# The first convolution block's projection, made in two halves among the last pair's attention

## The chip, the cores and the metric

The kernel runs on one core of a Trainium2 chip. The metric is the device time of one execution in microseconds (us). The core's engines are PE (TensorE, matrix products; PEld is its weight loading), DVE (VectorE), ACT (ScalarE), POOL (GpSimd) and SP, whose queue issues most of the transfers. Each works through its own list of instructions in order and waits for the others by semaphores. PE's products go to PSUM, eight banks of 128 x 512 floats; everything else lies in SBUF.

## What is computed

One layer of a streaming encoder on a sequence of 1024 tokens of width 1024, all in float32. Cut to what matters here:

```
h = rmsnorm(x) * (1 + scale_m(c)) + shift_m(c)
z, xbc, dt, q, k, v = split(h @ W_in)
xbc = silu(causal_dwconv(xbc, conv_w) + conv_b)      # 1024 channels, 4 taps
y_s = mamba2_ssd(xbc, dt) * silu(z), normed          # 8 heads x 64
y_a = chunked_attention(q, k, v, rel_bias)           # 8 heads x 64, own chunk and 8 before
x = x + gate_m(c) * (concat[y_s, y_a] @ W_out)
x = x + gate_f(c) * conv_ffn(rmsnorm(x) * (1 + scale_f(c)) + shift_f(c))
out = rmsnorm(x)
```

The change concerns the first 128 of the channels of xbc that the kernel treats first (block 4 of eight blocks): their projection `h @ W_in`, and the convolution behind it.

## The kernel before

**Precision.** Matrix products are made in three parts for float32 accuracy: each operand is split into a high part (a copy in a reduced format, on ACT) and a low part (the difference, on DVE or POOL). `mm3` (L83 to L86) issues high by high, high by low and low by high. `split` (L88 to L94) makes the parts. The normed input lies transposed in SBUF for the whole first phase as `hH` and `hL`, two halves of 512 tokens.

**Projection.** `gemm_ft` (L665) multiplies one block of 128 output channels with all tokens: for each half of the tokens, eight steps over the width, three matmuls of 512 columns each, so 24 matmuls a half and 48 a block. `wu_pair` (L156) loads a block's weights into one of two `raws` buffers, and splits them into `wh` (two buffers) and `wl` (one of two halves of one buffer, taken in turn).

**Attention.** `attention(p)` (L637) treats heads in four pairs. A pair has four steps u of two blocks of 128 queries. `attn_scores` (L567) makes the scores of both heads of one block in two PSUM tiles `s` (two buffers of two banks in all), adds the bias and takes the row maximum on DVE (L581), the exponential on ACT (L584), the reciprocal of the sum on DVE (L586) and the scaling on POOL (L587), into tiles `p` (eight buffers). `attn_pv` (L591) turns p on PE (L613, L616, into `tp`, two banks), splits it (ACT and DVE, L93, L94), and multiplies it with v into `pv` (one bank); L629 and L630 add its two parts into `ya`.

**The filler.** Between a step's scores and its pv part, `attention` calls the functions that the table `GP` (L34) lists for the pair and the step: projections of the q, k and v of the pairs to come, by `gemm_part` (L674). They accumulate in the tile `acc`, one bank (L686), and `evac_qkv` (L232) takes the result out: for v by a copy on ACT into a p tile (L259), for q and k by ACT and DVE (L243, L250, L253). `GPIN` ties some of these matmuls behind certain scores. In pair 3 the steps 0 and 1 have filler (the second token halves of k and v of pair 3 itself), and the steps 2 and 3 have none. In the steps 1 and 2 of pair 3 the weights of the convolution blocks 4 and 6 are loaded and split ahead of time into `early` (L660).

**Convolution stage.** After attention `conv_silu(ft)` (L694) treats the eight blocks in the order 4, 6, 5, 7, 0, 1, 2, 3. It takes an `s` tile (both halves of the tokens, L696), makes the projection (L697), starts the convolution with the last tap on ACT (L699), adds three taps on DVE, reading the projection in PSUM (L701), and applies silu on ACT (L705). After each block `conv_mods` (L749) makes up to four columns of modulation: a 512 KB weight load on SP (L144) into `xs` or `wos`, and a product with a row `rowa` that is summed on DVE (L146). The tiles of this stage lie in SBUF where attention's lay. Later come the z projection (L847, weights by `wz_weights`, L832), the SSD scan, the output projection and the feed-forward part.

**rowb.** `rowb` (L106) is a row buffer of 1024 floats a partition, beside `rowa` in one tile. Early on it holds a diagonal and then the first pair's bias, later (L769) a row of gates. Between pair 0 and L769 nothing uses it.

**Order.** The order of instructions on each engine is planned when the program is built: the framework lays the program out on a simulated timeline (L1807), taking what stands earlier in the program first among what is ready, unless `tc.issue_after` ties an instruction behind another. So a change in the program may alter the order elsewhere too. In the trace, parts of attention's pv work lie as late as 311 us, among the convolution's matmuls.

Of the kernel before, what the change touches and what calls it, by code (L numbers as in the profile page):

```python
# [10 lines left out]
F32 = mybir.dt.float32  # L11
F32R = mybir.dt.float32r
AF = mybir.ActivationFunctionType
# [3 lines left out]
P = 128  # L17
# [13 lines left out]
BOTH, H0, H1 = (0, 1), (0,), (1,)  # L31
# [1 line left out]
        (3, 2, H1): {0: (3, 0), 3: (3, 1), 6: (3, 2)}}  # L33
GP = {1: {0: ((2, 0, BOTH), (2, 1, BOTH)), 2: ((2, 2, BOTH),)},  # L34
      2: {0: ((3, 0, BOTH), (3, 1, H0)), 2: ((3, 2, H0),)},
      3: {0: ((3, 1, H1),), 1: ((3, 2, H1),)}}
XL = (3, 4, 7, 7)
XS = (4, 6, 7, 7)
XM = (6, 7, 7, 7)
# [33 lines left out]
def tile_block(ctx: ExitStack, tc: tile.TileContext, x, ccol, pk, w_ada, w_first, w_ft, w_z,  # L73
               w_out, w_up, w_down, bias, fnw, out, dbg=None):
    nc = tc.nc
    V, A, T = (InOrder(tc, e) for e in (nc.vector, nc.scalar, nc.tensor))
# [6 lines left out]
    def mm3(ps, lh, ll, rh, rl, start, stop, more=False):  # L83
        T.matmul(ps, lh, rh, start=start, stop=False, skip_group_check=more)  # L84
        T.matmul(ps, lh, rl, start=False, stop=False, skip_group_check=more)  # L85
        T.matmul(ps, ll, rh, start=False, stop=stop, skip_group_check=more)  # L86

    def split(hi, lo, src, ehi, elo, scale=None):  # L88
        if scale is not None:
            A.activation(hi, src, AF.Copy, scale=scale)  # L90
            V.scalar_tensor_tensor(lo, src, scale, f32(hi), op0=ALU.mult, op1=ALU.subtract)
            return
        i = A.activation(hi, src, AF.Copy) if ehi is A else ehi.tensor_copy(hi, src)  # L93
        return i, elo.tensor_tensor(lo, src, f32(hi), ALU.subtract)  # L94
# [11 lines left out]
    rowa, rowb = rows_[:, 0, :], rows_[:, 1, :]  # L106
# [32 lines left out]
    def raw_tile(n=1024):  # L139
        rawc[0] += 1  # L140
        return raws[:, rawc[0] % 2, 0:n]
# [14 lines left out]
    def wu_pair(src, hieng, loeng):  # L156
        t = raw_tile()
        nc.sync.dma_start(t, src)
        wh = wu.tile([P, 1024], F32R, tag="wh", name="wh")
        if not wls:  # L160
            wls.append(wu.tile([P, 2, 1024], F32R, tag="w2", bufs=1, name="wl"))
        wl = wls[0][:, rawc[0] % 2, :]
        split(wh, wl, t, hieng, loeng)
        return wh, wl
# [8 lines left out]
    def ht(hh, kt):  # L173
        return hth[hh][:, :, kt, :], htl[hh][:, :, kt, :]

    def c4(ap):
        return ap.rearrange("p (a b) -> p a b", a=4)
# [9 lines left out]
    psv = es_p1.enter_context(tc.tile_pool(name="psv", bufs=1, space=PSUM, reuse_waits="tile"))  # L187
# [35 lines left out]
    def new_pair(p):  # L223
        qk[p] = {n: [qk_tile(F32R) for _ in range(2)] for n in ("q", "kh", "kl")}
        qk[p]["v"] = vv[:, :, p % 2]
# [6 lines left out]
    def evac_qkv(p, which, hh, ps, tmp, tps):  # L232
        d = qk[p]
        c = slice(hh * 512, hh * 512 + 512)
        up, dn = slice(64, 128), slice(0, 64)

        def move(dst, o, src, r, sc):
            nc.sync.dma_start(f32(dst[o, c]), f32(src[r, sc]))

        if which == 0:  # L240
            q0, q1 = d["q"]
            lo = ev_tile()
            A.activation(q0[:, c], ps, AF.Copy, scale=0.125)  # L243
            V.scalar_tensor_tensor(lo, ps, 0.125, f32(q0[:, c]), op0=ALU.mult, op1=ALU.subtract)
            move(q1, up, q0, up, c)
            move(q1, dn, lo, up, slice(0, 512))
            move(q0, up, lo, dn, slice(0, 512))
        elif which == 1:
            (kh0, kh1), (kl0, kl1) = d["kh"], d["kl"]
            A.activation(kh0[:, c], ps, AF.Copy)  # L250
            for o in (up, dn):
                move(kh1, o, kh0, up, c)
            V.tensor_tensor(kl0[:, c], ps, f32(kh0[:, c]), ALU.subtract)  # L253
            for o in (up, dn):
                move(kl1, o, kl0, up, c)
            for t in (kh0, kl0):
                move(t, up, t, dn, c)
        else:
            A.activation(tmp, ps, AF.Copy)  # L259
            for j in range(4):  # L260
                T.transpose(tps[:, j * P:(j + 1) * P], tmp[:, j * P:(j + 1) * P], ident)
            b = slice(4 * hh, 4 * hh + 4)
            tv = tps.rearrange("p (a h b) -> p a h b", a=4, h=2)
            split(d["v"][:, b, :, 0, :], d["v"][:, b, :, 1, :], tv, A, V)

    def s_tile():
        return ps1.tile([P, 1024], F32, tag="s", bufs=2, name="s")
# [283 lines left out]
    def p_tile():  # L551
        return pp.tile([P, 640], F32, tag="p", name="p")

    def tp_tile():
        return pst.tile([P, 512], F32, tag="tp", bufs=2, name="tp")
# [78 lines left out]
    last_v, last_g, early = [], [], {}  # L634
# [30 lines left out]
    def gemm_ft(wh, wl, outs, pins={}, hhs=BOTH):  # L665
        for hh in hhs:
            for kt in range(KT):
                w = slice(kt * P, (kt + 1) * P)
                with tc.issue_after(slast[pins[kt]]) if hh == hhs[0] and kt in pins else ExitStack():
                    mm3(c4(outs[hh]), wh[:, w], wl[:, w], *ht(hh, kt), kt == 0, kt == KT - 1)  # L670

    held = {}

    def gemm_part(p, which, hhs):  # L674
        if which == 0:
            new_pair(p)
        if which == 2 and hhs == H1:
            wh, wl = held.pop(p)
        elif p == 2 and which < 2:
            with tc.issue_after(wpin[0].ins), tc.issue_after(wpin[1].ins):  # L680
                wh, wl = wu_pair(w_ft[8 + 3 * (p - 2) + which], A, V)
        else:
            wh, wl = wu_pair(w_ft[8 + 3 * (p - 2) + which], A, G)
        if which == 2 and hhs == H0:
            held[p] = wh, wl
        outs = {hh: psv.tile([P, 512], F32, tag="acc", bufs=1, name="acc") for hh in hhs}  # L686
        gemm_ft(wh, wl, outs, GPIN.get((p, which, hhs), {}), hhs)
        for hh in hhs:
            tmp = tps = None
            if which == 2:  # L690
                tmp, tps = p_tile()[:, 0:512], tp_tile()
            evac_qkv(p, which, hh, outs[hh], tmp, tps)

    def conv_silu(ft, dst):  # L694
        wh, wl = early.pop(ft) if ft in early else wu_pair(w_ft[ft], A, V)
        ps = s_tile()  # L696
        gemm_ft(wh, wl, [ps[:, 0:512], ps[:, 512:1024]])  # L697
        w = [pkt[:, SCW + 4 * ft + j:SCW + 4 * ft + j + 1] for j in range(4)]
        A.activation(dst, ps, AF.Identity, scale=w[3], bias=pkt[:, SCB + ft:SCB + ft + 1])  # L699
        for j in range(1, 4):  # L700
            last = V.scalar_tensor_tensor(dst[:, j:S], ps[:, 0:S - j], w[3 - j], dst[:, j:S],  # L701
                                          op0=ALU.mult, op1=ALU.add)
        for hh in range(2):
            c = slice(hh * 512, hh * 512 + 512)
            A.activation(dst[:, c], dst[:, c], AF.Silu)  # L705
        return last.ins

    part = lambda *a: (lambda: gemm_part(*a))
    bias_early()
    attention(0)  # L710
# [53 lines left out]
    for g in range(2):  # L764
        conv_mods(2 * g + 1, conv_silu(4 + g, bt_[g]))
        if g == 1:
            V.tensor_tensor(gcol[:, 0:8], modc[:, G_M:G_M + 8], gbias[0], ALU.add)
            cols_to_dram(gcol[:, 0:8], tp_tile()[0:8, 0:P], th512()[0:8, 0:P], gmd)
            for t, k in ((rowb[:, 0:512], 0), (gm1, 4)):  # L769
                nc.sync.dma_start(t.rearrange("p (a b) -> p a b", a=4), rows_from(gmd, k, 4))  # L770
        conv_mods(2 * g + 2, conv_silu(6 + g, ct_[g]))
# [5 lines left out]
    for ft in range(4):  # L777
        xt = bcp.tile([P, S], F32, tag="rm", bufs=2, name="xst")
        conv_mods(5 + ft, conv_silu(ft, xt))
        for hh in range(2):  # L780
            tps = tp_tile()
            for j in range(4):
                T.transpose(tps[:, j * P:(j + 1) * P], xt[:, (4 * hh + j) * P:(4 * hh + j + 1) * P],
                            ident)
            A.activation(xs[:, 4 * hh:4 * hh + 4, ft * P:(ft + 1) * P],
                         tps.rearrange("p (a b) -> p a b", a=4), AF.Copy)
# [698 lines left out]
    bufs = {}  # L1485
# [325 lines left out]
```

## Time and profile before

| | |
|---|---|
| median of 3 runs | 1171.44 us (1170.91 to 1171.88) |
| the profiled execution itself | 1171.69 us, span 1170.0 us |
| DVE, ACT, POOL busy | 78%, 50%, 13% of the span |
| chain that ended last, by engine | PE 86%, DVE 9%, ACT 3%, issue 2% |
| DMA packets | 64029, 169.15 MB, mean 145 GB/s |
| projection of block 4 on PE | from 248.07 to 262.25 us, in `s`, among pv work |
| its convolution on DVE | from 264.77 to 269.28 us |

The span runs from the first to the last instruction of the profiled execution. A line of the trace names start and duration in us, engine, line of the kernel, operation, and what is written from what. In a list of groups the number after "x" counts instructions, then come the busy time in us and the mean of one in ns, then the idle time of the engine just before them. In a list of waits, the engine and line that waited stand first, then the releaser, the time in all, how often, and the longest. A matmul is recorded with a modelled end: one of 512 columns shows about 390 ns, while the next may start 0.23 us after it.

### The profile page before, as it was taken

What the parts mean: (1) busy time and instruction counts of PE and PEld (TensorE: products, weight loads), DVE (VectorE), ACT (ScalarE), POOL (GpSimd) and SP (SyncE); (2) the same over time, 40 slices, a digit from 0 to 9 for tenths busy, and PEclk for the clock granted to TensorE, in tenths of its full rate; (3) what the DMA queues carried; (4) which work ended last, traced back from release to release, by engine and by line L of the source; (5) the groups of instructions that cost most, each with busy time, mean ns of one, the idle gap of its engine ahead of it and who ended that gap; (6) DMA issues with size and microseconds to landing.
All of it is one profiled execution on the core that took longest, in us unless ns stands there. A gap on an engine that the chain in (4) does not pass through costs nothing.

```text
span 1170.0 us, 15828 instructions
## 1 busy us (share of the span) xinstructions
PE 1151.2 (98%) x5849; PEld 975.0 (83%) x5849; DVE 909.3 (78%) x1360; ACT 585.5 (50%) x977; POOL 153.3 (13%) x179
## 2 busy tenths in 40 slices
PE   9999999999999999999999999999999999999997
PEld 7888888888889988887788888888888888888885
DVE  7836545588886688569999988899888869666986
ACT  5625555664345666586453444334443444433454
POOL 1103333430000356100000000000000000000622
PEclk9999999999999999999999999999999999999999
DMA  9835323145577622241323322232233378633444
GB/s 338 295 86 144 89 71 77 51 168 190 179 260 290 218 90 77 77 135 36 99 108 135 124 75 99 108 134 83 81 108 117 118 281 299 246 118 125 162 135 153
DMA packets 64029, 169.15 MB, mean 145 GB/s; under 512 B 6912, under 2 KB 7376, under 8 KB 62544
## 3 DMA queue, kind: packets, MB, share of 16 engines
q1 hardware_dynamic: 56608, 143.11, 36.8%
q10 hardware_dynamic: 7344, 25.04, 5.4%
q8 instruction: 46, 0.75, 0.3%
q14 instruction: 31, 0.25, 0.1%
HBM read 125.87 MB, written 32.81 MB: 136 GB/s over the span
## 4 chain that ended last, share of the span: by engine, by line
PE 86%; DVE 9%; ACT 3%; issue 2%; POOL 0%; POOLq 0%; ACTq 0%; DVEq 0%
PE wops L915 6%; PE dn L86 5%; PE dn L84 5%; PE dn L85 5%; PE uY L86 5%; PE uY L85 5%; PE uY L84 5%; PE uX L86 3%; PE uZ L85 3%; PE uZ L84 3%; PE uZ L86 3%; PE uX L85 3%; PE uX L84 3%; PE s L84 3%; PE s L86 3%; PE s L85 3%
## 5 line engine op out<-in xcount | busy, mean ns | idle before, releaser
L85 PE MATMUL dn<-w 128*128 128x512 f32 x296 | 107.4, 389 | 0.0
L84 PE MATMUL dn<-w 128*128 128x512 f32 x296 | 107.4, 389 | 0.0
L86 PE MATMUL dn<-w 128*128 128x512 f32 x296 | 99.8, 390 | 0.1
L84 PE MATMUL uY<-tH,w 128*128 128x512 f32 x248 | 96.5, 389 | 0.0
L86 PE MATMUL uY<-tH,w 128*128 128x512 f32 x248 | 96.5, 389 | 0.0
L85 PE MATMUL uY<-tL,w 128*128 128x512 f32 x248 | 96.5, 389 | 0.0
L1664 POOL TENSOR_TENSOR ya<-ya,xs 128x512 f32<-128x512 f32 x4 | 18.2, 4588 | 551.0 <-ACT xs L1660 551.0
L93 ACT ACTIVATE w<-ya 128x1024 fp32r<-128x1024 f32 (+1 forms) x41 | 39.1, 954 | 85.3 <-PE uY L86 75.2
L915 PE MATMUL wops<-hH,yhl 128*128 128x512 f32 x224 | 73.0, 398 | 1.1 <-DVE yhl L94 1.1
L86 PEld LDWEIGHTS dn<-w 128*128 128x128 f32 x296 | 55.4, 188 | 12.3 <-DVE w L94 0.8
L85 PEld LDWEIGHTS dn<-w 128*128 128x128 f32 x296 | 55.6, 188 | 11.6
L84 PEld LDWEIGHTS dn<-w 128*128 128x128 f32 x296 | 55.6, 188 | 11.5
L587 POOL TENSOR_SCALAR p<-p,st 128x640 f32<-128x640 f32 (+4 forms) x64 | 44.2, 699 | 112.0 <-DVE st L586 108.2
L93 ACT ACTIVATE w<-xs 128x1024 fp32r<-128x1024 f32 (+1 forms) x41 | 39.1, 954 | 37.1 <-PE uY L86 31.0
L581 DVE CUSTOM_DVE_ANT_0 p<-s,bias 128x640 f32<-128x640 f32 (+4 forms) x58 | 38.2, 675 | 23.7 <-PE tp L616 9.6
L84 PEld LDWEIGHTS uY<-tH,w 128*128 128x128 f32 x248 | 46.6, 188 | 9.7
L86 PEld LDWEIGHTS uY<-tH,w 128*128 128x128 f32 x248 | 46.6, 188 | 9.7
L94 DVE TENSOR_TENSOR pt<-tp,pt 128x512 fp32r<-128x512 f32 (+2 forms) x72 | 41.7, 596 | 16.5 <-ACT pt L93 16.2
L85 PEld LDWEIGHTS uY<-tL,w 128*128 128x128 f32 x248 | 46.6, 188 | 9.6
L1338 DVE SCALAR_TENSOR_TENSOR a<-cv,pkt,a 128x1023 f32<-128x1023 f32 (+1 forms) x40 | 51.0, 1278 | 0.1
L84 PE MATMUL s<-hH,wh 128*128 128x512 f32 x128 | 50.6, 395 | 0.1
L86 PE MATMUL s<-hH,wl 128*128 128x512 f32 x128 | 50.3, 393 | 0.0
(505 smaller groups left out, 3387.0 us busy)
## 6 DMA issues: line engine op xcount, KB each, us to landing
xs<-in_w_ada_dram SPq DMA_DIRECT2D x20, 512.0 KB, 4.7
gz<-a ACTq DMA_DIRECT2D x10, 1024.0 KB, 5.1
ya<-in_w_up_dram SPq DMA_DIRECT2D x11, 768.0 KB, 4.2
xs<-in_w_up_dram SPq DMA_DIRECT2D x11, 768.0 KB, 4.1
raws<-in_w_ft_dram SPq DMA_DIRECT2D x15, 512.0 KB, 4.0
adat<-in_w_ada_dram SPq DMA_DIRECT2D x14, 512.0 KB, 5.0
qk<-qk SPq DMA_DIRECT2D x56, 128.0 KB, 2.3
wos<-in_w_ada_dram SPq DMA_DIRECT2D x12, 512.0 KB, 4.6
```

The source lines that it names most:

```text
L84: T.matmul(ps, lh, rh, start=start, stop=False, skip_group_check=more)
L85: T.matmul(ps, lh, rl, start=False, stop=False, skip_group_check=more)
L86: T.matmul(ps, ll, rh, start=False, stop=stop, skip_group_check=more)
L93: i = A.activation(hi, src, AF.Copy) if ehi is A else ehi.tensor_copy(hi, src)
L94: return i, elo.tensor_tensor(lo, src, f32(hi), ALU.subtract)
L581: V.tensor_tensor_reduce(out=dst, in0=src, in1=bsl, scale=-1.0, scalar=3e38, op0=ALU.add, op1=ALU.min, accum_out=nm)
L587: last_g.append(G.tensor_scalar(pv_, pv_, rr, 1.0, op0=ALU.mult, op1=ALU.mult).ins)
L915: i = op(*a, **k)
L1338: V.scalar_tensor_tensor(a[:, j:S], c[:, 0:S - j], w[2 - j], a[:, j:S], op0=ALU.mult, op1=ALU.add)
L1664: G.tensor_tensor(src, src, fnr[:, halves[1]], ALU.mult)
```

## The change

Block 4's projection is taken out of the convolution stage. `GP` gets two more entries: in pair 3, step 2 calls `gemm_part(4)`, step 3 `gemm_part(5)`. These go to the new `conv_half`, for the first and the second half of the tokens: 24 matmuls into the tile `acc`, then a copy on ACT into a half of `rowb`. In the convolution stage `conv_silu(4)` takes no `s` tile and makes no projection, but reads `rowb`. Everything else of the block stays as it was.

```diff
       2: {0: ((3, 0, BOTH), (3, 1, H0)), 2: ((3, 2, H0),)},
-      3: {0: ((3, 1, H1),), 1: ((3, 2, H1),)}}
+      3: {0: ((3, 1, H1),), 1: ((3, 2, H1),), 2: ((4,),), 3: ((5,),)}}
...
-    def gemm_part(p, which, hhs):
+    def conv_half(hh):
+        ps = psv.tile([P, 512], F32, tag="acc", bufs=1, name="acc")
+        gemm_ft(*early[4], {hh: ps}, {}, (hh,))
+        A.activation(rowb[:, 512 * hh:512 * hh + 512], ps, AF.Copy)
+
+    def gemm_part(p, which=None, hhs=None):
+        if which is None:
+            return conv_half(p - 4)
         if which == 0:
             new_pair(p)
...
     def conv_silu(ft, dst):
-        wh, wl = early.pop(ft) if ft in early else wu_pair(w_ft[ft], A, V)
-        ps = s_tile()
-        gemm_ft(wh, wl, [ps[:, 0:512], ps[:, 512:1024]])
+        if ft == 4:
+            ps = rowb
+        else:
+            wh, wl = early.pop(ft) if ft in early else wu_pair(w_ft[ft], A, V)
+            ps = s_tile()
+            gemm_ft(wh, wl, [ps[:, 0:512], ps[:, 512:1024]])
```

## The prediction

> **What bounds the kernel now.** I read the page first, then the stretches around the last head pair's attention, then the waits and the groups of the one stretch that the change can fill, then single matmul starts.
>
> ```profile
> PE 1151.2 (98%) x5849; PEld 975.0 (83%) x5849; DVE 909.3 (78%) x1360; ACT 585.5 (50%) x977; POOL 153.3 (13%) x179
> ```
>
> TensorE (PE) is busy 98% of the span, so a move of matmuls can only win time in which PE stands. The next view splits the span into stretches (start:end, length, then each engine's busy time and count): an attention stretch with projection work as filler, the last pair's thin part, the stretch from 237.90 on, the convolution stage, and the z projection behind it.
>
> ```profile
> core 0: us, PE busy (x) PEld busy (x) DVE busy (x) ACT busy (x) POOL busy (x), PEclk, DMA share, GB/s
> 142.00:198.00 56.00, 55.66 (x329) 48.76 (x327) 28.36 (x81) 29.53 (x69) 18.42 (x24) 1.00 0.33 90
> 213.20:237.90 24.70, 21.80 (x146) 18.68 (x145) 15.28 (x48) 15.48 (x40) 9.44 (x13) 1.00 0.30 87
> 237.90:248.07 10.17, 9.90 (x67) 8.26 (x66) 9.74 (x30) 10.03 (x26) 5.42 (x8) 1.00 0.08 11
> 248.07:349.70 101.63, 101.63 (x508) 85.70 (x509) 86.23 (x125) 38.71 (x62) 4.98 (x6) 1.00 0.64 218
> 349.70:400.00 50.30, 50.30 (x423) 49.94 (x421) 32.38 (x59) 28.82 (x70) 2.72 (x2) 1.00 0.69 251
> ```
>
> With filler (142 to 198) PE stands 0.3 us in 56. Without enough of it (213.2 to 237.9) it stands 2.9 us in 24.7. From 248.07 to 400 it never stands: every microsecond of matmul that leaves this part ends it earlier, as long as nothing else becomes late. From 237.90 to 248.07 ACT (10.03 of 10.17) and DVE (9.74) are the full engines and PE follows them.
>
> **Where the new filler can start.** The halves are accumulated in the tile acc (one bank). Its last user before is the v projection of pair 3, and ACT takes that result out late, because (as I read the code) the copy's destination is one of the eight p tiles, which hold attention rows. The weights come from POOL.
>
> ```profile
> 237.34 0.58 ACT L259 ACTIVATE p<-acc 128x512 f32<-128x512 f32 x1
> ```
> ```profile
> 229.27 4.71 POOL L94 TENSOR_TENSOR wl<-raws,wh 128x1024 fp32r<-128x1024 f32 x2 [1.01 <-PE acc L86]
> ```
>
> The two low parts wl (block 4, then block 6) are ready by 234.0, the bank only at 237.9. So the 2.9 us of standing before 237.9 stay as they are, and the change can fill what stands between 237.9 and 248.07, where today the first matmul of the convolution's projection starts.
>
> **How much stands there.** A matmul's recorded end is modelled, so busy time hides short stops. I therefore add up the work by start distances. These are the PE groups of that stretch, and the starts from which I take the distances.
>
> ```profile
> L279 PE MATMUL s<-qk 128*128 128x320 f32 x26 | 5.4, 333 | 0.1
> L616 PE MATMUL tp<-ident,p 128*128 128x128 f32 x10 | 2.1, 272 | 0.0
> L613 PE MATMUL tp<-ident,p 128*128 128x128 f32 x7 | 1.9, 289 | 0.0
> L624 PE MATMUL pv<-pt,v 128*128 128x256 f32 x5 | 1.5, 323 | 0.1
> L625 PE MATMUL pv<-pt,v 128*128 128x256 f32 x5 | 1.3, 283 | 0.0
> L625 PE MATMUL pv<-pt,v 128*128 128x128 f32 x5 | 1.3, 265 | 0.0
> L624 PE MATMUL pv<-pt,v 128*128 128x128 f32 x4 | 1.0, 238 | 0.0
> L261 PE MATMUL tp<-ident,p 128*128 128x128 f32 x4 | 0.6, 273 | 0.0
> ```
> ```profile
> 236.76 1.42 PE L279 MATMUL s<-qk 128*128 128x320 f32 x8
> 238.01 0.22 PE L625 MATMUL pv<-pt,v 128*128 128x128 f32 x1
> ...
> 241.44 0.28 PE L625 MATMUL pv<-pt,v 128*128 128x256 f32 x1
> 241.56 0.22 PE L624 MATMUL pv<-pt,v 128*128 128x128 f32 x1
> 241.62 0.28 PE L625 MATMUL pv<-pt,v 128*128 128x128 f32 x1
> ...
> 242.07 0.27 PE L613 MATMUL tp<-ident,p 128*128 128x128 f32 x1
> 242.18 0.27 PE L616 MATMUL tp<-ident,p 128*128 128x128 f32 x1
> ...
> 248.07 0.50 PE L84 MATMUL s<-hH,wh 128*128 128x512 f32 x1
> 248.41 0.40 PE L85 MATMUL s<-hL,wh 128*128 128x512 f32 x1
> ...
> 253.41 0.40 PE L86 MATMUL s<-hH,wl 128*128 128x512 f32 x1
> ```
>
> Eight 320-column matmuls take 238.01 - 236.76 = 1.25, so 0.156 each; a 256-column one takes 0.12, a 128-column pv one 0.06, a transpose 0.11. The groups then need 26 x 0.156 + 10 x 0.12 + 9 x 0.06 + 21 x 0.11 = 4.06 + 1.20 + 0.54 + 2.31 = 8.1 us. The stretch is 10.17 us long, so about 2.0 us of it is standing: the upper bound of what can be filled there. The recorded idle time, 10.17 - 9.90 = 0.27, is the lower one. The waits with a named releaser lie between them:
>
> ```profile
> PEld s L279 <- DVE st L581: 1.0, 5, 0.3
> PEld pv L624 <- DVE ya L630: 0.3, 1, 0.3
> PEld s L84 <- DVE st L581: 0.2, 1, 0.2
> ```
>
> These 1.5 us are waits for DVE, which other matmuls can cover. The other 0.5 us are the short stops when a weight load could not run ahead, and those come back at each change of work: at 248.07 the step to the next matmul is 0.34 us, where it is 0.23 further on.
>
> **The change, part by part.** (1) *48 matmuls move.* From 248.41 to 253.41 lie 22 steps, 0.227 us each, so 48 are 10.9 us. They leave the convolution stage and come between the scores, transposes and pv products from 237.9 on. Their own cost is nil, PE runs them anyway; what counts is the standing that they cover. I take the 1.5 us of named waits, and 0.1 us off for the break between the halves: 1.4 us. (2) *Two copies on ACT.* Each is a 128x512 copy out of acc, as L259 above: 0.58 us, 1.2 in all, on an engine that is full there. What queues behind them are exponentials, and behind these the pv transposes. Their cover is the moved work itself: the 8.1 + 10.9 = 19 us of PE work against 10.03 + 1.2 = 11.2 of ACT. I cost them at nothing; without that cover they would cost 1.2. (3) *The convolution reads SBUF instead of PSUM.* The first row below reads PSUM, the second SBUF:
>
> ```profile
> L701 DVE SCALAR_TENSOR_TENSOR bt<-s,pkt,bt x6: 1261/1280/1283, 264.8 to 292.6; 128x1023 f32<-128x1023 f32 x2, 128x1022 f32<-128x1022 f32 x2, 128x1021 f32<-128x1021 f32 x2
> ```
> ```profile
> L1338 DVE SCALAR_TENSOR_TENSOR a<-cv,pkt,a x40: 1271/1278/1296, 568.9 to 914.2; 128x1023 f32<-128x1023 f32 x20, 128x1022 f32<-128x1022 f32 x20
> ```
>
> 1280 against 1278 ns: nothing. The chain can run as soon as the second half is copied, and it holds no s tile, so later blocks get theirs earlier. (4) *Weights.* The block's wh buffer comes free earlier, so the next block's split starts earlier; no loss. (5) *The SP queue.* The change issues no transfer. But two loads in that queue wait for attention, and attention gets 10.9 us of work in between:
>
> ```profile
> SPq L144 <- PE s L279: 11.7, 1, 11.7
> SPq L144 <- PE pv L625: 8.5, 1, 8.5
> ```
>
> The first (modulation weights into xs, after the last scores) may come up to 10.9 us later. DVE, which works on them, has 101.63 - 86.23 = 15.4 us to spare up to 349.7, so I cost it at nothing. The second is the rival on the slower side, below.
>
> Sum: 1.4 us out of PE's standing, and since PE stands nowhere from 248 to 400, it should arrive at the end. The profiled execution took 1171.69 us with a span of 1170.0 us, so it would take 1170.3; the median of the runs is 1171.44, which gives **1170.0 us**. A measurement of this kernel can tell about 0.2%, 2.3 us, from no change; the forecast lies within that.
>
> **Rivals.**
>
> *Nothing is filled (1171.2).* The 48 matmuls may land behind the last scores, where the same 48 lie now, and only the recorded 0.27 us goes. For it: the stretch is short and the halves stand behind two pairs of scores in program order. Against it: from 142 to 198 projection work did go into the gaps. [...]
>
> *More is filled (1167.9).* The order of every engine is planned anew. If the bank is emptied earlier, filler also reaches the 2.9 us of standing before 237.9: 2.0 plus half of 2.9 is 3.5 us; all of both would give 1166.5. Against it: nothing in the change frees a p tile sooner.
>
> *The one bank (1172.5).* The second half cannot start before ACT has copied the first. If nothing stands between the halves in PE's order, PE waits for the last matmul's end (0.40), the copy (0.58), and what ACT has ahead of it, two exponentials:
>
> ```profile
> 248.05 0.83 ACT L584 ACTIVATE p<-p,st 128x640 f32<-128x640 f32 x1
> ```
>
> 0.40 + 0.58 + 2 x 0.83 = 2.6 us, less the 1.5 won: 1.1 slower. With nothing won it is 1174.0. [...]
>
> *Attention's tail comes too late (1174.5).* This is the one on the other side. The second SP row shows modulation loads (into wos) held until the last pv product; behind them in the same queue stand the z weights. The rows are the last pv product, the last z weight split on ACT, and the first z matmul.
>
> ```profile
> 311.29 0.27 PE L625 MATMUL pv<-pt,v 128*128 128x128 f32 x1
> ```
> ```profile
> 340.39 0.64 ACT L93 ACTIVATE wzh<-raws 128x520 fp32r<-128x520 f32 x1 [1.14 <-DMA raws<-in_w_z_dram]
> ```
> ```profile
> 349.57 0.28 PE L84 MATMUL zps<-wzh,hH 128*128 128x260 f32 x1
> ```
>
> The hi part is done at 341.0; the lo part on DVE adds about 0.7 us (an estimate, 520 of the 1024 columns of the convolution row above), so the cover is 349.57 - 341.7 = 7.8 us. If the halves merely push attention back, the tail comes the whole 10.9 us later while z wants to start as before, and PE stands 10.9 - 7.8 = 3.1 us: 1174.5. It decides from a tail later by 7.8 us. Against it: the tail is already spread thinly among the convolution matmuls, at the pace of DVE rather than of PE.
>
> **How the numbers follow.** Forecast 0.44, nothing filled 0.18, more filled 0.16, one bank 0.10, late tail 0.12. The forecast's own spread goes from 1169.4 (all 2.0 us) to 1171.2, with a shift of the plan elsewhere on top; I give a quarter of its chance, 0.11, to a time under 1169.1. Faster is then 0.16 + 0.11 = 0.27; slower is 0.12, 0.04 of the one bank, and 0.02 for a plan that comes out worse elsewhere, 0.18; within 0.2% 0.55. The range reaches from 1167.0, most of "more filled", to 1174.5, the late tail; outside I leave about 0.10 to 0.15.
>
> **What would show it.** Right: acc matmuls of the moved block between 238 and about 258, two copies of acc into rows of some 0.58 us, DVE waits of score weight loads in that part down from 1.0 us, and the z projection's first matmul 1 to 2 us earlier than 349.57. Wrong: a wait of PE for the copy between the halves; the z weights' split becoming the last wait ahead of z; a first z matmul that comes no earlier; or a gain that is there at 349 and gone by 540, where the scan's order was planned anew.

## The result and the profile after

| | time, us | ratio to before | last pv product starts | first tap of block 0 starts |
|---|---|---|---|---|
| before | 1171.32 (1170.91 to 1172.01, 6 runs) | 1 | 311.29 | 315.15 |
| after | 1179.39 (1178.0 to 1180.7, 6 runs) | 1.0071 [1.0061, 1.0080] | 320.48 | 321.20 |

The change makes the kernel 8 us slower, outside the range that was predicted. The profiled execution of the changed kernel took 1180.7 us, its span is 1179.0. In its line numbers L699, L701, L705 and L783 have become L709, L711, L715 and L793; the new copy is L677.

The page's busy shares do not show the loss. PE has the same 98% as before:

```profile
PE 1152.5 (98%) x5849; PEld 976.6 (83%) x5849; DVE 908.6 (77%) x1360; ACT 586.9 (50%) x979; POOL 152.3 (13%) x179
```

The same stretches as in the prediction (start:end, length, busy time and count of PE, weight load, DVE, ACT, POOL, then the granted PE clock, the DMA share and GB/s) show where it is:

```profile
213.20:237.90 24.70, 22.21 (x149) 19.26 (x149) 15.28 (x49) 15.49 (x39) 10.06 (x13) 1.00 0.29 83
237.90:248.07 10.17, 10.17 (x63) 9.17 (x62) 6.85 (x20) 7.47 (x19) 3.15 (x5) 1.00 0.00 0
248.07:349.70 101.63, 96.92 (x489) 81.45 (x488) 80.26 (x122) 39.59 (x65) 5.71 (x8) 0.98 0.61 208
349.70:400.00 50.30, 47.58 (x363) 45.89 (x362) 33.92 (x61) 22.82 (x52) 0.00 (x0) 0.97 0.63 218
```

From 237.90 on the halves fill PE (10.17 of 10.17, weight loads 9.17 instead of 8.26), while DVE falls from 9.74 to 6.85 and ACT from 10.03 to 7.47: the attention work now waits behind the halves. Then comes what there was none of before: PE stands idle for 4.7 us in the convolution stage and 2.7 us in the z stage, with a granted clock of 0.98 and 0.97.

The local part of the change works. The timeline of ACT has the two copies of the halves and, right behind the second, the first tap that reads them:

```profile
246.78 0.57 ACT L677 ACTIVATE rows<-acc 128x512 f32<-128x512 f32 x1
257.80 0.57 ACT L677 ACTIVATE rows<-acc 128x512 f32<-128x512 f32 x1
258.40 1.25 ACT L709 ACTIVATE bt<-rows,pkt 128x1024 f32<-128x1024 f32 x1
```

The last matmul of block 1's projection is a good mark, because both kernels have by then the same PE instructions behind them. Before it starts at

```profile
325.55 0.39 PE L86 MATMUL s<-hH,wl 128*128 128x512 f32 x1
```

and after at 322.03, 3.5 us earlier. These are PE's rows of the changed kernel around it:

```profile
320.48 0.28 PE L625 MATMUL pv<-pt,v 128*128 128x128 f32 x1
...
322.03 0.39 PE L86 MATMUL s<-hH,wl 128*128 128x512 f32 x1
322.98 0.39 PE L84 MATMUL zps<-wzh,hH 128*128 128x260 f32 x1 [0.56 <-ACT wzh L93]
...
329.09 0.79 PE L84 MATMUL s<-hH,wh 128*128 128x512 f32 x1 [3.25 <-DVE xst L711]
329.68 0.63 PE L85 MATMUL s<-hL,wh 128*128 128x512 f32 x1
330.11 0.63 PE L86 MATMUL s<-hH,wl 128*128 128x512 f32 x1
```

So PE arrives 3.5 us early, and the next block's projection starts at 329.09, 6.8 us after the place where it would follow (322.03 + 0.23); only twelve z matmuls, 1.4 us, lie in between. This stretch of 6.8 us is called the stand from here on. The waits that PE has from 290 to 380 us (before it has none there; name of the waiting line, releaser, total, times, longest):

```profile
PE s L84 <- DVE xst L711: 3.2, 1, 3.2
PE tp L793 <- ACT xst L715: 1.7, 1, 1.7
PE s L84 <- ACT zs L868: 1.0, 1, 1.0
PE zps L85 <- DVE wzl L94: 0.9, 1, 0.9
PE zps L84 <- ACT wzh L93: 0.6, 1, 0.6
```

The first says what holds PE: block 2 needs an s tile, both are full with blocks 0 and 1, and DVE has not finished the taps that empty the first. The waits for the z weights (the last two rows) lie inside the stand. Why it hasn't finished can be read on ACT and DVE. The tail of attention on ACT, before and after:

```profile
311.60 0.38 ACT L629 ACTIVATE tl<-pv 64x256 f32<-64x256 f32 x1 [2.66 <-PE pv L625]
312.00 0.27 ACT L151 ACTIVATE th<-tp 8x128 f32<-8x128 f32 x1
314.19 1.06 ACT L93 ACTIVATE wh<-raws 128x1024 fp32r<-128x1024 f32 x1 [1.91 <-PE s L85]
315.15 1.19 ACT L699 ACTIVATE xst<-s,pkt 128x1024 f32<-128x1024 f32 x1
```
```profile
315.17 0.27 ACT L151 ACTIVATE th<-tp 8x128 f32<-8x128 f32 x1
320.79 0.38 ACT L629 ACTIVATE tl<-pv 64x256 f32<-64x256 f32 x1 [5.35 <-PE pv L625]
321.20 1.21 ACT L709 ACTIVATE xst<-s,pkt 128x1024 f32<-128x1024 f32 x1
```

Before, block 0's first tap follows its own projection, 3.2 us after the end of tl, and its three DVE taps run on without a break:

```profile
316.42 3.91 DVE L701 SCALAR_TENSOR_TENSOR xst<-s,pkt,xst 128x1023 f32<-128x1023 f32 x3
```

After, the first tap stands right behind the last piece of attention, though block 0's projection has long been done. DVE has nothing to do meanwhile and too much afterwards. Its rows after, and three finer stretches, before and after:

```profile
321.21 0.42 DVE L630 TENSOR_TENSOR ya<-pv,tl 64x256 f32<-64x256 f32 x1 [5.51 <-ACT tl L629]
322.44 1.28 DVE L711 SCALAR_TENSOR_TENSOR xst<-s,pkt,xst 128x1023 f32<-128x1023 f32 x1 [0.81 <-ACT xst L709]
323.64 0.69 DVE L94 TENSOR_TENSOR wzl<-raws,wzh 128x520 fp32r<-128x520 f32 x1
324.25 1.28 DVE L711 SCALAR_TENSOR_TENSOR xst<-s,pkt,xst 128x1022 f32<-128x1022 f32 x1
325.44 1.22 DVE L94 TENSOR_TENSOR wl<-raws,wh 128x1024 fp32r<-128x1024 f32 x1
326.57 2.47 DVE L711 SCALAR_TENSOR_TENSOR xst<-s,pkt,xst 128x1023 f32<-128x1023 f32 x2
```
```profile
311.00:322.00 11.00, 11.00 (x53) 8.97 (x52) 8.33 (x12) 3.19 (x5) 0.00 (x0) 1.00 0.62 215
322.00:330.00 8.00, 8.00 (x41) 6.73 (x40) 7.22 (x11) 4.42 (x7) 0.00 (x0) 1.00 0.88 305
330.00:340.00 10.00, 10.00 (x50) 8.35 (x49) 8.97 (x14) 4.39 (x7) 0.00 (x0) 1.00 0.65 217
```
```profile
311.00:322.00 11.00, 11.00 (x56) 9.05 (x55) 1.32 (x3) 1.76 (x4) 0.00 (x0) 1.00 0.27 76
322.00:330.00 8.00, 3.29 (x16) 2.36 (x15) 7.56 (x7) 3.36 (x5) 0.00 (x0) 0.94 0.73 261
330.00:340.00 10.00, 10.00 (x44) 8.22 (x44) 10.00 (x18) 3.45 (x8) 0.00 (x0) 0.88 0.83 267
```

DVE goes from 8.33 to 1.32 busy in 311 to 322, and is full from 330 to 340. Among its taps of block 0 stand two weight splits, 0.69 and 1.22 us as recorded, which prolong the chain that PE waits for. And behind the stand the clock is lower: the 512-column matmuls at 329.68 and 330.11 are 0.43 us apart, where the step is 0.23 otherwise. The granted clock is 0.50 from 329.02 to 332.43, and 0.50 once more from 369.99 to 373.40, behind the two shorter waits in the z stage (1.0 and 1.7 us).

By the end the loss is complete: the last z matmul starts at 407.38 instead of 398.32, 9.06 us later, and the span is 9.0 us longer. The scan and the feed-forward part neither add nor give back anything.

### The profile page after: what moved, and what is told of

Its sections match the earlier page's. It is cut to its first block, busy times and chain, and to the rows that moved or that the text cites. A ratio compares the mean times of both kernels' runs of the same rounds, so it can differ in the third digit from the quotient of the medians.

```text
span 1179.0 us, 15822 instructions
## 1 busy us (share of the span) xinstructions
PE 1152.5 (98%) x5849; PEld 976.6 (83%) x5849; DVE 908.6 (77%) x1360; ACT 586.9 (50%) x979; POOL 152.3 (13%) x179
## 4 chain that ended last, share of the span: by engine, by line
PE 82%; DVE 11%; ACT 2%; issue 2%; DMA 2%; SPq 0%; POOL 0%; POOLq 0%; ACTq 0%; DVEq 0%
PE wops L925 6%; PE dn L86 5%; PE dn L85 5%; PE dn L84 5%; PE uY L86 5%; PE uY L84 5%; PE uY L85 5%; PE uX L86 3%; PE uZ L84 3%; PE uZ L86 3%; PE uZ L85 3%; PE uX L84 3%; PE uX L85 3%; PE acc L85 3%; PE acc L84 3%; PE acc L86 3%
## 5 line engine op out<-in xcount | busy, mean ns | idle before, releaser
L93 ACT ACTIVATE pt<-tp 128x512 fp32r<-128x512 f32 (+2 forms) x72 | 36.7, 525 | 28.5 <-PE tp L613 14.9
L925 PEld LDWEIGHTS wops<-hH,yhl 128*128 128x128 f32 x224 | 41.9, 188 | 10.1 <-DVE yhl L94 1.9
```

Of the source, the lines that this page charges most:

```text
L925: i = op(*a, **k)
```

## The experiments

Theory: attention's last pv product comes 9.2 us later, and block 0's convolution waits for it; the stand and the clock follow from that. Rivals: the copies and the SBUF operand; the later last scores; the wos loads and z weights, as the prediction's last rival had it; and for the size, the clock or DVE. Where no tie is added, calling the halves behind the step's pv part, or behind all of attention, leaves the planned order of every engine as it was, instruction for instruction. So for these calls it is not true that what stands earlier in the program goes first, as the section on the kernel before has it; in the versions below the order is moved by ties (`issue_after`).

**Copies alone.** The kernel before, with

```diff
+        if ft == 4:
+            for hh in range(2):
+                A.activation(rowb[:, 512 * hh:512 * hh + 512], ps[:, 512 * hh:512 * hh + 512], AF.Copy)
+            ps = rowb
```

> The kernel before, with one part of the change: block 4 keeps its projection in the convolution stage and in an s tile, and two ACT copies bring it to rowb, from which it is convolved. Theory (the last pv product of attention comes too late, and with it the first x block, the wos loads and the z weights): no halves stand among attention, so no loss, 1170 to 1172 us, last pv product no later than 311.3. Rival (the copies and the reading of SBUF cost it): most of the 8 us, 1177 to 1180.

Measured: 1171.29 us, ratio 1.0005 [0.9996, 1.0015]. The copies and the SBUF operand cost nothing that shows; the loss is not theirs. In this version attention ends even earlier than before, and that brings nothing:

```profile
299.70 0.27 PE L625 MATMUL pv<-pt,v 128*128 128x128 f32 x1
```

**No half, or one half, ahead of the last scores.** Both from the changed kernel, with the halves called in `conv_silu(4)` and tied as follows:

```diff
-        gemm_ft(*early[4], {hh: ps}, {}, (hh,))
+        gemm_ft(*early[4], {hh: ps}, ({0: (3, 7)}, {})[hh], (hh,))      # behind_scores
+        gemm_ft(*early[4], {hh: ps}, ({}, {0: (3, 7)})[hh], (hh,))      # one_ahead
```

> The change, with the first half tied behind the last scores (3,7), so that no half stands ahead of any score. In PE's planned order 264 projection matmuls stand ahead of the last pv group (before: 230, changed kernel: 281). Theory (the last pv product's time decides): it comes at 311.3 + 34 x 0.227 = about 319, so still slow, 1175 to 1179. Rival (the delay of the last scores, and of the modulation loads that wait for them, decides): scores end near 246 again and the time is back at 1170 to 1172.

> The change, with only the second half tied behind the last scores (3,7); the first half stands ahead of the last two scores as in the changed kernel. In PE's planned order 234 projection matmuls stand ahead of the last pv group (before: 230). Theory (the last pv product's time decides): it comes at about 311 again, and the time is 1169 to 1172 although the last scores are late by some 5 us. Rival (the late scores decide): about half of the loss, 1174 to 1176.

Measured: 1172.25 us, 1.0014 [1.0005, 1.0024], and 1169.26 us, 0.9988 [0.9979, 0.9997]. First the row of the last pv product and PE's one wait of behind_scores, then the pv row and the SP wait for the last scores of one_ahead:

```profile
317.50 0.27 PE L625 MATMUL pv<-pt,v 128*128 128x128 f32 x1
```
```profile
PE s L84 <- DVE xst L713: 1.4, 1, 1.4
```
```profile
309.75 0.27 PE L625 MATMUL pv<-pt,v 128*128 128x128 f32 x1
```
```profile
SPq L144 <- PE s L279: 16.3, 1, 16.3
```

With one half ahead the last scores are 4.6 us later than before (16.3 against 11.7), and the kernel is 1.6 us faster than before: the late scores do no harm. With none ahead the scores come as before (SP waits 11.7 again), yet the last pv product is 6.2 us later than before, and PE waits for the same xst, 1.4 us. The two runs speak for the place of the last pv product and against the scores. Its price I had overrated: of the 1175 to 1179 expected, 1172.25 came. The theory had no threshold in it: with the last pv product at 317.5, block 0's chain is only 1.4 us late for PE.

**The tail pulled forward.** The changed kernel, with two ties in `gemm_ft` behind pv products:

```diff
+PVPIN = {7: {0: (3, 3, 0)}, 0: {0: (3, 3, 1)}}
...
-            gemm_ft(wh, wl, [ps[:, 0:512], ps[:, 512:1024]])
+            gemm_ft(wh, wl, [ps[:, 0:512], ps[:, 512:1024]], PVPIN.get(ft, {}))
...
```

> The change as it is, both halves where they were, with two more ties: block 7's projection starts behind the pv products of step 3's first head, block 0's projection behind those of its second head. In PE's planned order the last pv group stands behind 192 projection matmuls (changed kernel: 281). Theory (the late last pv product makes the loss): it comes near 300, the whole loss goes and the local gain of about 2 us stays: 1168.5 to 1171. Rival 1 (the late scores, the copies or the acc bank cost it): 1178 to 1180 still. Rival 2 (PE now stands for DVE's and ACT's part of the pv work): 1172 to 1176.

Measured: 1176.74 us, 1.0053 [1.0038, 1.0068], nearest to the second rival and a little above its range. The last pv product comes at 307.69 and PE is busy without a break from 300 to 376, but PE, tied to attention, now waits for DVE in front of it:

```profile
PE pv L625 <- DVE ya L631: 2.1, 1, 2.1
PE pv L626 <- DVE pt L95: 1.6, 1, 1.6
```

From 248 to 300 PE is busy 48.21 of 52.00 us at a clock of 0.97. An early end of attention must not be bought with a wait on PE. This run moved the loss and could not tell its cause.

**xst elsewhere.** ACT's rows leave open whether block 0's first tap came late because tl stood ahead of it in ACT's order, or because its memory was not free. In the changed kernel as built, v takes bytes 147392 to 163775 of each partition, and the two xst tiles begin at 157632 and 161728: they lie on v, which the last pv product reads. A pool of their own puts them at 167872 and 171968, where q and k of the last pair lay:

```diff
+    rmp = es_b.enter_context(tc.tile_pool(name="rmp", bufs=1, side="right", reuse_waits="tile"))
     bcp = es_b.enter_context(tc.tile_pool(name="bcp", bufs=1, side="right", reuse_waits="tile"))
...
-        xt = bcp.tile([P, S], F32, tag="rm", bufs=2, name="xst")
+        xt = rmp.tile([P, S], F32, tag="rm", bufs=2, name="xst")
```

(the same for `woh` and `cr`, later tiles that share these two buffers; three tiles of the scan, `xdt`, `xdd` and `cb`, shift with it, and no other tile of the convolution or the z stage).

> The changed kernel, with the tiles xst (and the later woh and cr) in a pool of their own, so that they lie where the last pair's q and k lay (free since the last scores, 255 us) and no longer where v lay, which the last pv product reads. PE's planned order up to the last pv product is the same, so attention ends as late as in the changed kernel, at about 320.5; the wos loads still wait for it. Theory (the late end of attention costs the time through the memory of xst): block 0's first tap starts near 310 instead of 321.2, DVE has work between 311 and 322, the stand of 3.2 us ahead of block 2 is gone, 1169 to 1172 us. Rival 1 (the late wos loads and z weights make the larger part, as the prediction's last rival had it): 1174 to 1178. Rival 2 (the late pv product only goes with another cause): 1178 to 1180.

Measured: 1169.97 us, 0.9992 [0.9983, 1.0002]. Its last pv product, its first tap, and two of the stretches:

```profile
321.43 0.28 PE L625 MATMUL pv<-pt,v 128*128 128x128 f32 x1
```
```profile
310.84 1.19 ACT L709 ACTIVATE xst<-s,pkt 128x1024 f32<-128x1024 f32 x1
```
```profile
311.00:322.00 11.00, 11.00 (x58) 9.08 (x57) 5.34 (x5) 2.98 (x6) 0.00 (x0) 1.00 0.22 74
322.00:330.00 8.00, 8.00 (x40) 6.66 (x39) 5.51 (x8) 3.88 (x6) 0.00 (x0) 1.00 0.87 301
```

Attention ends even later than in the changed kernel, at 321.43; the wos loads still wait for it and are issued at 321.77. But block 0's first tap starts at 310.84, in front of attention's end, PE is full from 311 to 340, the waits of 3.2, 1.7 and 1.0 us are gone (the longest left on PE from 231 to 400 us is 0.7), and with them the whole loss, 9.4 us. So the memory under xst carries the loss, and the late wos loads and z weights do not. ACT works through a planned order in both versions; the move lets the plan put the tap ahead of tl. The control and the best version with the same move:

> Control: the kernel before with the same move of xst alone, in which the last pv product comes at 311.3, ahead of the end of block 0's projection. Every theory: within 1 us of the kernel before, 1170 to 1172; a gain of more would mean that the place of xst helps by itself.

> The version with one half ahead of the last scores (1169.3 us) with xst moved as well. Theory (its attention ends at about 310 already, in time): the same as without, 1168.5 to 1170. If its first tap still waited for v by a little: up to 1 us less.

Measured: 1170.83 us, 0.9997 [0.9988, 1.0007], and 1169.07 us, 0.9982 [0.9973, 0.9991]. The place of xst is worth nothing where attention ends in time (310.58 and 310.10).

**The clock.** Empty matmuls in PE's stand, ahead of block 2:

```diff
+            if ft == 2:
+                wm = psv.tile([P, 512], F32, tag="pv", bufs=1, name="warm")
+                with tc.issue_after(T.mm):          # block 1's last matmul
+                    for _ in range(44):             # stand_covered: 22
+                        i = T.matmul(wm[:, 0:P], ident, ident, start=True, stop=True)
+            with tc.issue_after(i.ins) if ft == 2 else ExitStack():
+                gemm_ft(wh, wl, [ps[:, 0:512], ps[:, 512:1024]])
...
```

> The changed kernel, with 44 empty matmuls (identity by identity, 128 columns, into the free pv bank; their result is not used) on PE between the projections of blocks 1 and 2, that is in the stand from 322.4 to 329.1. They take 44 x 0.11 = 4.8 us of a stand of 6.6; the 12 z matmuls that stood there (1.4 us) move behind. The theory that the lower granted clock behind the stand (0.88 from 330 to 340) comes from PE's standing: clock 0.99 or more there, the 512-column step back at 0.227 us, 1.2 us less there, against 1.4 us of z matmuls later: 1178 to 1180 in all. Rival (the clock falls for another cause): 0.88 again, and 1180 to 1182.

Measured: 1179.18 us, 1.0068 [1.0053, 1.0083], with the clock at 1.00 all along. But my duration was wrong: each showed as two records of 0.11 us, so that the 44 took 9.7 us and lay about 3 us over the stand's end (block 2 starts at 332.24, in the changed kernel at 329.09). That PE lost these 3 us more, and the time stayed the same, already suggests that the clock had cost about as much. Half of them measure it:

> The changed kernel once more, to stand beside the next one on the same chip: 1178 to 1181 us.

> The changed kernel with 22 empty matmuls in the stand in place of 44 (in the run before each showed as two records of 0.113 us, so 44 took 9.8 us and lay over the stand's end). 22 take 5.0 us, from 322.5 to 327.5, then the 12 z matmuls (1.4 us) as in the changed kernel, then block 2 at 329.1: the stand is covered and not prolonged, and PE's order is the changed kernel's. Theory (part of the loss is the lower granted clock that follows the stand): 0.99 or more from 322 to 340, and 1 to 3 us less than the changed kernel. Rival (DVE is the bound behind the stand, busy 10.00 of 10.00 us from 330 to 340, so a faster PE only waits later): clock 0.99 or more, time within 0.5 us of the changed kernel.

Measured: the changed kernel again 1179.68 us, 1.0075 [1.0060, 1.0090]; with the stand covered 1175.28 us, 1.0038 [1.0023, 1.0053]. PE's rows at the stand, and the stretch behind it, first covered, then in the changed kernel of the same set:

```profile
322.60 5.07 PE L713 MATMUL warm<-ident 128*128 128x128 f32 x44
...
329.44 0.50 PE L86 MATMUL s<-hH,wh 128*128 128x512 f32 x1 [0.33 <-DVE xst L720]
329.77 0.40 PE L87 MATMUL s<-hL,wh 128*128 128x512 f32 x1
330.01 0.39 PE L88 MATMUL s<-hH,wl 128*128 128x512 f32 x1
```
```profile
330.00:340.00 10.00, 10.00 (x50) 8.35 (x49) 10.00 (x18) 4.34 (x8) 0.00 (x0) 1.00 0.82 263
```
```profile
330.00:340.00 10.00, 10.00 (x39) 8.09 (x39) 10.00 (x15) 3.46 (x7) 0.00 (x0) 0.76 0.72 251
```

Block 2 starts no earlier (329.44, against 329.09 and, in the second profile of the changed kernel, 329.70), but the next steps are 0.24 us instead of 0.43, and 4.4 us are saved by matmuls that compute nothing (by the medians; the two profiled executions are 3.3 us apart). The rival, that DVE would be the bound behind the stand and a faster PE would only wait, is false, although DVE is 10.00 of 10.00 busy there. The 4.4 us is more than the 1 to 3 expected. In the second profile of the changed kernel the granted clock is 0.50 from 328.05 to 334.88 (the stretches 322 to 330 and 330 to 340 show 0.88 and 0.76), and PE has matmuls for 5.2 us of that. At steps of 0.23 instead of 0.43 the same matmuls would take 2.8 us, so about 2.4 us (an estimate from these figures) is the clock itself. How the rest of the 4.4 us comes about is not shown. The granted clock was 0.50 for 3.41 us twice in the first profile of the changed kernel, and for 6.83 us once in the second. PE did not stand all the time ahead of such a drop: the one at 369.99 in the first profile came although PE was busy 1.69 of the 3.40 us ahead of it, and tail_pulled, where PE's longest wait is 2.1 us, has a granted clock of 0.97 from 248 to 300. How much standing it takes, no run here shows.

**A version that keeps the gain.** One half spread between the scores, and xst elsewhere: `({0: (3, 4), 2: (3, 5), 4: (3, 6), 6: (3, 7)}, {})[hh]`.

> A version meant to keep the gain: the first half in four parts tied behind the scores (3,4) to (3,7), the second half behind it, and xst moved away from v. PE's planned order has the last pv group behind 234 projection matmuls. Theory: last pv product near 310, no stand ahead of block 2, the local gain of about 2 us kept: 1168.5 to 1170. If spreading the first half costs the cover of the score waits: up to 1171.5.

Measured: 1169.90 us, 0.9991 [0.9982, 1.0001]. No better than one half ahead. Whether it differs from one_ahead_xst can't be told, as the intervals overlap.

## Why the prediction was wrong

- **Where the filler starts, and how much it fills (right in place, small in size).** The bank came free at 237.2, the first matmul in acc starts at 237.84. None of the 1.5 us of named waits from 237.9 on is left. The gain was put at 1.4 us, with 2.0 as its upper bound; at block 1's end PE is 3.5 us ahead. Part of that lies ahead of 237.9, where PE's busy time rose from 21.80 to 22.21 by the new order; the rest is not split up. 3.5 us is also what the rival *more is filled* gave, but by 1.5 us of filling ahead of 237.9, of which 0.4 shows, so that match is chance. In the version with one half ahead, block 1's last matmul starts at 322.62, 2.9 us ahead of before, and the span of its profiled execution is 2.7 us shorter (1.6 us by the medians): there a good part of the gain does arrive at the end.
- **Nothing is filled (false).** Weight loads rose by 0.9 us in that stretch (8.26 to 9.17), and the version that keeps the gain is 1.6 us faster.
- **Copies and the SBUF operand at nothing (right).** Copies of 0.57 us, DVE taps of 1.281 us against 1.280, and copies_only at a ratio of 1.0005.
- **The one bank (false).** PE has no wait for the copy. Between the halves (246.07 to 248.23) it has scores and pv work.
- **The mods loads up to 10.9 us later, at nothing (right).** SP's wait for the last scores is 9.7 us longer than the 11.7 of before, and xst_elsewhere, which keeps this wait as it is, loses nothing by it:

```profile
SPq L144 <- PE s L279: 21.4, 1, 21.4
```

- **"Since PE stands nowhere from 248 to 400, it should arrive at the end" (the step that failed).** That PE doesn't stand says that its operands come in time now, and not by how much. The cover of a tile is the time from the end of the work on it to the moment when PE needs that work done; for block 0's xst it was 5.4 us before (taps until 320.33, block 1's projection until 325.78). Two things ate it at once: the halves pushed attention's end back by 9.2 us, and the gain pulled PE forward by 3.5. The first tap of block 0 had started 3.2 us after tl, and its chain (1.19 + 3.91 us) has to end by the time that block 1's projection does. With that end at 322.26, the tap had to start by 317.2; it started at 321.20, and 1.9 us of weight splits came into the chain: 4.0 + 1.9 = 5.9 of the 6.8 us. The sign that the prediction named for being right, a first z matmul 1 to 2 us earlier than 349.57, shows nothing here: it starts at 322.98, but as one of the twelve that the plan puts between blocks 1 and 2.
- **The late tail (the right rival, with the wrong victim and a third of the price).** Its place and its kind were right: a last pv product later by more than 7.8 us. But I followed the SP queue to the z weights, because that wait has a row. The reader that counts, xst on v's memory, had none, since that wait never ended last before the change. And 3.1 us of standing left out what a stand does to the clock: covering it took back 4.4 of the 8.7 us. At 0.12 the rival was also given too little.

What stays open: why the planner sets the last pv group behind 281 projection matmuls in the changed kernel, 264 in behind_scores and 234 in one_ahead, against 230 before. The runs show what its place does, and not what moves it.

## What to carry to other kernels

Where a move delays the end of a stage, list what the next stage writes onto that stage's memory, and take the cover of each such tile; a wait that has no row today may be the one that ends last tomorrow. The cover shrinks from both sides, by the delay and by the gain. Price a stand of TensorE together with the clock behind it (here 0.50 for 3.41 us in one profile and 6.83 in another; covering the stand took back 4.4 of the 8.7 us), and try first whether another place in SBUF takes the dependence away: here four lines were worth the whole loss.

## What the runs showed of the hardware

- Half of the loss came back by 22 empty matmuls (4.4 of 8.7 us): behind a stand of 6.8 us with 1.4 us of work in it, 512-column matmuls came every 0.43 us instead of 0.23, with a granted clock of 0.50 for 3.41 us in one profile and 6.83 us in a second.
- PE did not stand all the time ahead of every such drop: in the changed kernel's first profile the clock also fell to 0.50 at 369.99, for 3.41 us, after 3.40 us in which PE was busy for 1.69.
- In stand_covered an empty matmul (identity by identity, float32, 128 columns) shows as two records and takes 0.22 us by the starts (22 matmuls, 44 records, from 322.60 to 327.43), while a transpose of 128 columns in the kernel before is one record and takes 0.11 (from 242.07 to 242.18).
